# Delta-rule stage of a two-block kernel: convolution scratch, gate logarithm, Newton steps and low halves on other tiles and engines

## Chip, cores and metric

One core of a Trainium2 chip runs the whole program. The metric is the device time of one execution in microseconds (us). Three executions of the kernel before took 1437.9, 1439.62 and 1441.2 us; their median is 1439.62 us. Five engines work side by side, each through its own queue in order: TensorE (PE), VectorE (DVE), ScalarE (ACT), GpSimd (POOL) and SyncE (SP), which issues the loads of the weights.

## What is computed

Two blocks of a network over 256 tokens of width 1024, in float32. The first is a WKV mixer with a feed-forward part, the second a gated delta rule with a multiscale pool, followed by an expert layer (PEER). The change lies almost wholly in the delta rule of the second block:

```python
qkv = silu(causal_conv(qkv, conv_w))          # 4 taps, 3 x 512 channels
q, k = l2norm(q), l2norm(k)                   # 4 heads of 128
beta = sigmoid(b_gate)
g = -exp(a_log) * softplus(a_dec + dt_bias)   # the gate, 8 numbers a token row
# per chunk
g = cumsum(g); decay = exp(g_i - g_j)
t_mat = triangular_solve(I + strict(k_beta k^T * decay), I)
v_new = t_mat v_beta - (t_mat k_beta e^g) state
o = (q e^g) state + (q k^T * decay) v_new
state = state * e^{g_last} + k_decay^T v_new
# after it
o = rmsnorm(o) * silu(z);  x = x + [o, pool] @ w_out
```

## The kernel before

Activations lie with channels on the 128 partitions and the 256 tokens along the row. Every weight tile (128x1024) is multiplied in split precision: a rounded high half `whi` (line 210, ACT) and the rest as a low half `wlo` (line 223, DVE or POOL), so that a projection is 8 x 3 = 24 matmuls of 128x256 (lines 366 to 368). `Stream.split` makes both halves of the next weight tile; its argument says which engine makes the low half. Three buffers of each half exist, and two more after `widen` (line 238), which the feed-forward part calls (line 1194).

`delta` (from line 1230) is the stage of the change. Its work is two generators that `weave` (line 264) interleaves. `main` (line 1490) is the chain of the delta rule: `head` with the four convolutions of k and the gate (lines 1345 to 1357), the gate's running sum and decay (1495 to 1513), the norm of k (`rsqrt_steps`, line 400: a bit trick and three Newton steps), the matrix `N` (1529 to 1532), its inverse in 16-wide blocks (`inverse16`, from 589: 15 steps of a product, line 620, and a row sum, line 623), three levels of merging (1554 to 1610), then the two chunks (1611 to 1635). `filler` (line 1431) is everything that does not depend on the chain: 16 projections, four each for q, v, the pool `p` and the gate `z`, the convolutions that follow them (`conv_ops`, line 1278), the pool's windows (1406), and four steps of the output projection. `main` yields a number of microseconds from the list `YL`, and the filler is advanced by so much; a scheduler then sets each engine's order by priority and by its own estimate of times. So the order on an engine depends on these numbers, on which engine an operation is given to, and on which buffers must come free.

- `conv_ops` writes the scaled input to a tile `ct` (four buffers, line 1282) and the tanh to `th` (four buffers, line 1273). The four convolutions of k hold all four `ct` until their third tap; the first convolution of q takes the next.
- `gate_ops` (1299 to 1343) computes softplus through a series of log1p in `l8`, on 128x8 numbers, mostly on DVE.
- The last norm, of `o`, is `rsqrt_steps` again (line 1643), and the spreads of its result (line 1656) and the last four output steps wait for it.

`DSP`, `DSZ` and `GO` (lines 1384, 1385, 1450) name the engine of the low halves in the filler: before, POOL for all of them.

Of the kernel before, what the change touches and what calls it, by code (L numbers as in the profile page):

```python
# [9 lines left out]
F32 = mybir.dt.float32  # L10
# [5 lines left out]
AF = mybir.ActivationFunctionType  # L16
ALU = mybir.AluOpType
PSUM = bass.MemoryType.PSUM
P = 128
T = 256  # L20
# [142 lines left out]
NAR = 3  # L163
WX = 2
TY = [1.20, 8.92]
YL = [0.56, 0.64, 1.60, 3.20, 0.64, 0.72, 0.48, 0.80, 0.40, 1.92, 1.20, 0.16]
LEAD2 = 3000
LEAD3 = 3000
DSZ = 2
ORD = "qvpz"  # L170
FPRE = ["pb", "pa"]
DSP = 2
TOPK = 1.5
GSPLIT = 3
# [113 lines left out]
class Builder:  # L288
# [108 lines left out]
    def rsqrt(self, *a, **k):  # L397
        return drive(self.rsqrt_steps(*a, **k))

    def rsqrt_steps(self, src, n, mult, add=None, floor=None, out=None, pace=0.2):  # L400
        nc, sm = self.nc, self.s1
        V = nc.vector
        v, y, t = (sm.tile([P, 16], F32, name=k, tag=k)[:, 0:n] for k in ("rv", "ry", "rt"))
        y = y if out is None else out
        short = n <= 2 and floor is None
        k = 2.0 ** -28 if short else 1.0
        magic = 0x5EB759DF - 2 ** 31 if short else 0x5F3759DF
        parts = min(n, 2)
        w = n // parts
        cut = [tuple(ap[:, k * w:k * w + w] for ap in (src, v, y, t)) for k in range(parts)]  # L410
        cut = [(sp, vp if mult else sp, yp, tp) for sp, vp, yp, tp in cut]
        for sp, vp, yp, tp in cut if mult else []:
            if floor is not None:
                V.tensor_scalar(vp, sp, mult, floor, ALU.mult, ALU.max)
            else:
                V.tensor_scalar(vp, sp, mult * k, add * k, ALU.mult, ALU.add)
        yield pace
        for sp, vp, yp, tp in cut:
            V.tensor_single_scalar(yp.bitcast(I32), vp.bitcast(I32), 1, ALU.logical_shift_right)
        yield pace  # L420
        for sp, vp, yp, tp in cut:
            V.tensor_scalar(yp.bitcast(I32), yp.bitcast(I32), -1, magic, ALU.mult, ALU.add)
        if short:
            for c in (0.75, 0.1875, 3.0 / 1024):
                for sp, vp, yp, tp in cut:
                    V.scalar_tensor_tensor(tp, yp, vp, yp, ALU.mult, ALU.mult)
                for sp, vp, yp, tp in cut:
                    V.scalar_tensor_tensor(yp, tp, -c, yp, ALU.add, ALU.mult)
            return y
        for _ in range(3):  # L430
            yield pace
            for sp, vp, yp, tp in cut:
# [728 lines left out]
    def ffn(self, xs, pre, rs):  # L1161
        tc, nc, S = self.tc, self.nc, self.S
        V, A = nc.vector, nc.scalar
        with tc.tile_pool(name="ffn", bufs=1) as fp:
# [23 lines left out]
            for j in range(22):  # L1188
                fg = conv(j, nextp())
                if j == 6:  # L1190
                    self.delta_consts(fg[:, 0:1])
                fu = conv(22 + j, nextp())
                if j == 10:
                    S.widen(WX, self.nc.gpsimd)
                if j > 1:
                    acc = acc or [self.pa() for _ in range(4)]
                    self.out_step(acc, prev.pop(0), j == 2, False)
                    S.split()
                A.activation(fg, fg, AF.Gelu_apprx_tanh)
                V.tensor_tensor(fg, fg, fu, ALU.mult)  # L1200
                ah = fp.tile([P, T], F32R, name="ah", tag="ah", bufs=3)
                al = fp.tile([P, T], F32R, name="al", tag="al", bufs=3)
                self.split(ah, al, fg)
                prev.append((ah, al))
# [25 lines left out]
    def delta(self, xs, pre, rs):  # L1230
        tc, nc, i, S = self.tc, self.nc, self.i, self.S
        x = self.x
        V, A, G = nc.vector, nc.scalar, nc.gpsimd
        mm = nc.tensor.matmul
        b4 = lambda ps: ps.rearrange("p (c s) -> p c s", c=4)
        with tc.tile_pool(name="del", bufs=1) as dp:
            t4 = lambda n, dt=F32, tag=None: dp.tile([P, 4, T], dt, name=n, tag=tag or n)
            wpl, wbh, wbl, ab = self.wpl, self.wbh, self.wbl, self.ab
            ea = self.ea
            self.region.close()  # L1240
            for n in range(3):
                S.split((G, V, V)[n])
            k, q, v = t4("k"), t4("q"), t4("v")
            pp = t4("pp")
            z = t4("z")
            tri = self.con("tri")
            st = {}

# [17 lines left out]
                S.split(eng)  # L1266
                return ps

            def silu_ops(dst, src):
                d = {}  # L1270

                def tanh():
                    d["th"] = dp.tile([P, T], F32, name="th", tag="th", bufs=4)
                    A.activation(d["th"], src, AF.Tanh, scale=0.5)

                return tanh, lambda: V.scalar_tensor_tensor(dst, d["th"], 1.0, src, ALU.add, ALU.mult)

            def conv_ops(dst, ps, ch):
                d = {}

                def first():
                    d["t"] = dp.tile([P, T], F32, name="ct", tag="ct", bufs=4)
                    V.tensor_tensor(d["t"], ps, rs, ALU.mult)  # L1283
                    A.activation(dst, d["t"], AF.Copy, scale=self.par("conv2", 36 + ch))

                def tap(s):
                    V.scalar_tensor_tensor(dst[:, s:T], d["t"][:, 0:T - s], self.par("conv2", (3 - s) * 12 + ch),
                                           dst[:, s:T], ALU.mult, ALU.add)

                tanh, last = silu_ops(dst, dst)  # L1290
                return [first, lambda: tap(1), lambda: tap(2), lambda: (tap(3), tanh()), last]

            sp = dp.tile([P, 2, 8], F32, name="sp")
# [5 lines left out]
            def gate_ops():  # L1299
# [12 lines left out]
                                yr.unsqueeze(2).to_broadcast([P, 2, 8]), ALU.mult)  # L1312
                A.activation(beta, sp[:, :, 0:4], AF.Exp, scale=-1.0)
                yield
                V.tensor_tensor(z8, sp[:, :, 4:8], ab[:, 1:2, :].to_broadcast([P, 2, 4]), ALU.add)
                yield
                V.scalar_tensor_tensor(e8, z8, -1.0, z8, ALU.mult, ALU.min)
                A.activation(e8, e8, AF.Exp)
                yield
                V.tensor_scalar(beta, beta, 1.0, None, ALU.add)  # L1320
                V.tensor_scalar(z8, z8, 0.0, None, ALU.max)
                yield
                V.tensor_scalar(w8, e8, 2.0, None, ALU.add)
                V.reciprocal(beta, beta)
                yield
                V.reciprocal(w8, w8)
                V.tensor_scalar(bh, beta, 0.5, None, ALU.mult)
                yield
                V.tensor_tensor(e8, e8, w8, ALU.mult)
                yield  # L1330
                V.tensor_tensor(w8, e8, e8, ALU.mult)
                yield
                V.tensor_scalar(l8, w8, 1.0 / 15, None, ALU.mult)
                for n in (13, 11, 9, 7, 5, 3):
                    yield
                    V.scalar_tensor_tensor(l8, l8, 1.0 / n, w8, ALU.add, ALU.mult)
                yield
                V.scalar_tensor_tensor(l8, l8, 1.0, e8, ALU.add, ALU.mult)
                yield
                V.scalar_tensor_tensor(l8, l8, 2.0, z8, ALU.mult, ALU.add)  # L1340
                yield
                V.scalar_tensor_tensor(gt.rearrange("p (b h) -> p b h", b=2), l8, -1.0, ea.to_broadcast([P, 2, 4]),
                                       ALU.mult, ALU.mult)

            def head():
                V.tensor_scalar(dnh, self.par("dn"), 0.5, None, ALU.mult)
                go = gate_ops()
                next(go)
                kc = [conv_ops(k[:, h, :], ps, 4 + h) for h, ps in enumerate(pre)]
                for n in range(5):  # L1350
                    for ops in kc:
                        ops[n]()
                        if n:
                            next(go, None)
                        yield YL[0]
                for _ in go:
                    yield 0.2
# [113 lines left out]
            att = dp.tile([P, 8, P], F32, name="att", tag="Y2")  # L1471
            vb = dp.tile([P, 8, P], F32, name="vb")
            kd = dp.tile([P, 4, P], F32, name="kd")
            vn = dp.tile([P, 8, P], F32, name="vn")
            Sx = dp.tile([P, 4, P], F32, name="Sx")
            o = t4("o")
            oh, ol = t4("oh", F32R, "dec"), t4("ol", F32R, "N")

            G.memset(Y, 0.0)
# [10 lines left out]
            def main():  # L1490
# [23 lines left out]
                ss = self.pc()  # L1514
                l2sums(k, ss)
                yield YL[1]
                yield from self.rsqrt_steps(ss[:, 0:8], 8, 1.0, 4e-6, out=yk, pace=YL[11])
                V.tensor_tensor(byk, beta.rearrange("p b h -> p (b h)"), yk, ALU.mult)
                gk = [b4(self.pa()), b4(self.pa())]
                for tb in range(2):  # L1520
# [490 lines left out]
```

## Time and profile before

| | |
|---|---|
| runs of the kernel before | 1437.9, 1439.62, 1441.2 us |
| the profiled execution, its time | 1440.79 us |
| its span, first to last instruction | 1439.0 us |
| PE busy | 1356.5 us (94%) |
| DVE busy | 1022.3 us (71%) |
| ACT busy | 683.1 us (47%) |
| POOL busy | 322.6 us (22%) |
| delta stage, first gate product to the last sum into x | 433.5 to 588 us |

Busy time is the time in which an engine has an instruction in work; it counts an instruction that is held up as busy. The line PEclk of the page gives the TensorE clock that was granted, as a share of 2.4 GHz: 1.00 is 2.4 GHz and 0.50 is 1.2 GHz. In the timeline a row is a start, a length, an engine, a line of the code and what is written from what. Neighbouring rows of one engine overlap a little in the record, so what an instruction costs in a full queue is the distance from its start to the next start.

### The profile page before, as it was taken

What the parts mean: (1) busy time and instruction counts of PE and PEld (TensorE: products, weight loads), DVE (VectorE), ACT (ScalarE), POOL (GpSimd) and SP (SyncE); (2) the same over time, 40 slices, a digit from 0 to 9 for tenths busy, and PEclk for the clock granted to TensorE, in tenths of its full rate; (3) what the DMA queues carried; (4) which work ended last, traced back from release to release, by engine and by line L of the source; (5) the groups of instructions that cost most, each with busy time, mean ns of one, the idle gap of its engine ahead of it and who ended that gap; (6) DMA issues with size and microseconds to landing.
All of it is one profiled execution on the core that took longest, in us unless ns stands there. A gap on an engine that the chain in (4) does not pass through costs nothing.

```text
span 1439.0 us, 26837 instructions
## 1 busy us (share of the span) xinstructions
PE 1356.5 (94%) x10570; PEld 1264.0 (88%) x10570; DVE 1022.3 (71%) x2072; ACT 683.1 (47%) x1241; POOL 322.6 (22%) x232
## 2 busy tenths in 40 slices
PE   7989999999997887999979999999999999999998
PEld 6888989999987787999879999999998888888886
DVE  6865768888869876799992777777875555555554
ACT  3522455565554422465444554444444544554454
POOL 4511341210044632202341000000002222222221
PEclk9899999999999898999999999999999999999999
DMA  6231434665523211345435444444446655666653
GB/s 219 63 98 46 147 118 151 208 214 182 189 90 132 88 45 59 134 159 164 162 133 184 155 160 147 147 147 148 147 151 202 196 197 192 192 194 198 192 191 118
DMA packets 64318, 217.88 MB, mean 151 GB/s; under 512 B 10272, under 2 KB 11232, under 8 KB 64064
## 3 DMA queue, kind: packets, MB, share of 16 engines
q1 hardware_dynamic: 59376, 212.76, 44.9%
q0 software_dynamic: 976, 2.71, 0.7%
q8 instruction: 83, 1.36, 0.4%
q10 hardware_dynamic: 3840, 0.70, 0.4%
q14 instruction: 43, 0.35, 0.1%
HBM read 214.69 MB, written 1.44 MB: 150 GB/s over the span
## 4 chain that ended last, share of the span: by engine, by line
PE 69%; DVE 23%; issue 3%; ACT 2%; POOL 2%; DMA 1%; SPq 0%; ACTq 0%; DVEq 0%
PE pa L1919 24%; PE pb L366 10%; PE pb L368 9%; PE pb L367 9%; DVE wlo L223 5%; PE pa L367 2%; PE pa L366 2%; PE pa L368 2%; POOL wlo L223 1%; DVE x L1862 1%; DVE scr L1683 1%; DVE eg L1866 1%; PE pb L1873 1%; PE pa L1562 1%; DVE scr L1684 1%
## 5 line engine op out<-in xcount | busy, mean ns | idle before, releaser
L210 ACT ACTIVATE whi<-raw 128x1024 fp32r<-128x1024 f32 x396 | 418.2, 1058 | 555.6 <-PE pb L367 261.0
L223 DVE TENSOR_TENSOR wlo<-raw,whi 128x1024 fp32r<-128x1024 f32 x346 | 426.5, 1233 | 253.4 <-ACT whi L210 248.3
L366 PE MATMUL pb<-xnh,whi 128*128 128x256 f32 x1024 | 296.9, 290 | 13.8 <-DVE scr L1847 8.3
L368 PE MATMUL pb<-xnh,wlo 128*128 128x256 f32 x1024 | 290.7, 285 | 11.5 <-POOL wlo L223 6.8
L367 PE MATMUL pb<-xnl,whi 128*128 128x256 f32 x1024 | 290.1, 284 | 0.0
L1919 PE MATMUL pa<-whi,up 128*128 128x512 f32 x1024 | 274.5, 389 | 0.0
L1919 PEld LDWEIGHTS pa<-whi,up 128*128 128x128 f32 x1024 | 192.2, 188 | 39.8
L366 PEld LDWEIGHTS pb<-xnh,whi 128*128 128x128 f32 x1024 | 196.7, 192 | 18.2 <-PE pb L368 12.9
L368 PEld LDWEIGHTS pb<-xnh,wlo 128*128 128x128 f32 x1024 | 196.6, 192 | 13.2 <-POOL wlo L223 7.3
L223 POOL TENSOR_TENSOR wlo<-raw,whi 128x1024 fp32r<-128x1024 f32 x55 | 145.3, 2649 | 259.5 <-ACT whi L210 245.2
L367 PEld LDWEIGHTS pb<-xnl,whi 128*128 128x128 f32 x1024 | 196.9, 192 | 0.0
L366 PE MATMUL pb<-xh,whi 128*128 128x256 f32 x648 | 188.8, 291 | 4.3 <-DVE ct L1283 4.1
L368 PE MATMUL pb<-xh,wlo 128*128 128x256 f32 x648 | 185.6, 286 | 1.3 <-DVE wlo L223 1.3
L367 PE MATMUL pb<-xl,whi 128*128 128x256 f32 x648 | 186.0, 287 | 0.4
L1919 PE MATMUL pa<-wlo,up 128*128 128x512 f32 x512 | 158.2, 389 | 0.0
L494 POOL TENSOR_TENSOR up<-hb,up 128x256 fp32r<-128x256 f32 x32 | 45.9, 1435 | 409.3 <-ACT up L493 409.3
L366 PEld LDWEIGHTS pb<-xh,whi 128*128 128x128 f32 x648 | 125.2, 193 | 5.7 <-issue 4.3
L368 PEld LDWEIGHTS pb<-xh,wlo 128*128 128x128 f32 x648 | 124.8, 193 | 1.8 <-DVE wlo L223 1.5
L367 PEld LDWEIGHTS pb<-xl,whi 128*128 128x128 f32 x648 | 125.0, 193 | 1.4 <-DVE xl L560 1.0
L1919 PEld LDWEIGHTS pa<-wlo,up 128*128 128x128 f32 x512 | 96.1, 188 | 19.9
L494 POOL TENSOR_TENSOR up<-scr,up 128x256 fp32r<-128x256 f32 x32 | 47.1, 1472 | 127.0 <-ACT up L493 127.0
L367 PE MATMUL pa<-al,whi 128*128 128x256 f32 x176 | 49.0, 281 | 0.0
(529 smaller groups left out, 2267.0 us busy)
## 6 DMA issues: line engine op xcount, KB each, us to landing
raw<-down SPq DMA_DIRECT2D x128, 512.0 KB, 3.3
raw<-up SPq DMA_DIRECT2D x128, 512.0 KB, 4.3
raw<-w_in SPq DMA_DIRECT2D x46, 512.0 KB, 3.3
raw<-w_up SPq DMA_DIRECT2D x44, 512.0 KB, 3.6
raw<-w_down SPq DMA_DIRECT2D x22, 512.0 KB, 3.4
raw<-w_out SPq DMA_DIRECT2D x16, 512.0 KB, 3.3
raw<-w_query SPq DMA_DIRECT2D x16, 512.0 KB, 3.3
x<-xT SPq DMA_DIRECT2D x4, 256.0 KB, 5.3
```

What stands on the lines that cost most here:

```text
L210: nc.scalar.activation(hi, self.raw[self.nh], AF.Copy)
L223: e.tensor_tensor(lo[:, a:z], raw[:, a:z], hi[:, a:z], ALU.subtract)
L366: mm(ps, w[0], x[0], start=start, stop=False, **k)
L367: mm(ps, w[0], x[1], start=False, stop=False, **k)
L368: mm(ps, w[1], x[0], start=False, stop=stop, **k)
L494: (eng or self.nc.vector).tensor_tensor(lo, src, hi.bitcast(F32), ALU.subtract)
L1562: mm(out[:, h], lh[:, tb * 4 + h, :], self.halves(rh[:, tb * 4 + h, :], l, odd), start=True, stop=True)
L1683: V.max_index(idx[:, 0:8], vals[:, 0:8], src)
L1684: V.match_replace(t, vals[:, 0:8], src, NEG)
L1862: V.tensor_tensor(e1, iota, over(self.i1t), ALU.is_equal)
L1866: V.tensor_tensor(eg[m], eg[0], over(self.gp[m]), ALU.mult)
L1919: mm(acc[tb * 2 + hf], a[:, ts], b[:, hf * 512:hf * 512 + 512], start=False, stop=(e == 127 and lo == 1), skip_group_check=True)
```

## The change

- The four convolutions of k no longer use `ct` and `th`. Their scaled input lies in `vn` and their tanh in `o`, two tiles that the chain fills only much later.
- The gate's series becomes 22 POOL instructions on 128x8 numbers, with two reciprocals, one product and `bh` left on DVE and the cut at zero moved to ACT.
- The three Newton steps of the norm of k become 12 POOL instructions on 128x8 numbers (the argument `eng`); the norm of `o` stays as it was.
- All low halves of the filler are made by DVE (`DSZ`, `DSP`, `GO`), as is the first of three at the stage's start and the two of `widen` in the feed-forward part.
- `YL[0]`, the filler's share for each step of the k convolutions, goes from 0.56 to 0.2.

```diff
-YL = [0.56, 0.64, 1.60, 3.20, 0.64, 0.72, 0.48, 0.80, 0.40, 1.92, 1.20, 0.16]
+YL = [0.2, 0.64, 1.60, 3.20, 0.64, 0.72, 0.48, 0.80, 0.40, 1.92, 1.20, 0.16]
-DSZ = 2
+DSZ = 0
-DSP = 2
+DSP = 0
-GO = "GGGG"
+GO = "VVVV"
...
     def rsqrt_steps(self, src, n, mult, add=None, floor=None, out=None, pace=0.2, eng=None):
...
+        if eng:
+            v = v if mult else src
+            for _ in range(3):
+                yield pace
+                eng.tensor_tensor(t, v, y, ALU.mult)
+                eng.tensor_tensor(t, t, y, ALU.mult)
+                eng.tensor_scalar(t, t, -0.5, 1.5, ALU.mult, ALU.add)
+                eng.tensor_tensor(y, y, t, ALU.mult)
+            return y
...
-                    S.widen(WX, self.nc.gpsimd)
+                    S.widen(WX, V)
...
-                S.split((G, V, V)[n])
+                S.split(V)
...
+            o = t4("o")
+            vn = dp.tile([P, 8, P], F32, name="vn")
...
-                    d["t"] = dp.tile([P, T], F32, name="ct", tag="ct", bufs=4)
+                    d["t"] = dp.tile([P, T], F32, name="ct", tag="ct", bufs=4) if ct is None else ct
...
-                V.tensor_tensor(e8, e8, w8, ALU.mult)
-                yield
-                V.tensor_tensor(w8, e8, e8, ALU.mult)
-                yield
-                V.tensor_scalar(l8, w8, 1.0 / 15, None, ALU.mult)
-                for n in (13, 11, 9, 7, 5, 3):
-                    yield
-                    V.scalar_tensor_tensor(l8, l8, 1.0 / n, w8, ALU.add, ALU.mult)
...
+                G.tensor_tensor(e8, e8, w8, ALU.mult)
+                G.tensor_tensor(w8, e8, e8, ALU.mult)
+                G.tensor_scalar(l8, w8, 1.0 / 15, 1.0 / 13, ALU.mult, ALU.add)
+                yield
+                for n in (11, 9, 7, 5, 3, 1):
+                    G.tensor_tensor(l8, l8, w8, ALU.mult)
+                    G.tensor_scalar(l8, l8, 1.0 / n, None, ALU.add)
+                G.tensor_tensor(l8, l8, e8, ALU.mult)
...
+                vt = vn.rearrange("p (h a) t -> p h (a t)", h=4)
+                kc = [conv_ops(k[:, h, :], ps, 4 + h, vt[:, h, :], o[:, h, :]) for h, ps in enumerate(pre)]
...
-                yield from self.rsqrt_steps(ss[:, 0:8], 8, 1.0, 4e-6, out=yk, pace=YL[11])
+                yield from self.rsqrt_steps(ss[:, 0:8], 8, 1.0, 4e-6, out=yk, pace=YL[11], eng=G)
```

The order on POOL after the gate. `egb` and `N`, `dec` are the decay tiles, `pw` and `pp` the pool's windows, `rt`, `rv` and `yk` the norm of k. Before:

```order
L223 TENSOR_TENSOR wlo<-raw,whi 128x1024 x9
L1586 TENSOR_TENSOR egb<-egb,q 128x512
L1507 TENSOR_TENSOR N<-dec,con_del 128x512 x2
L1533 TENSOR_TENSOR dec<-dec,con_del 128x512
L223 TENSOR_TENSOR wlo<-raw,whi 128x1024
L1533 TENSOR_TENSOR dec<-dec,con_del 128x512
L1410 TENSOR_TENSOR pw<-pp 128x255
```

And now:

```order
L1590 TENSOR_TENSOR egb<-egb,q 128x512
L1416 TENSOR_TENSOR pw<-pp 128x255
L434 TENSOR_TENSOR rt<-rv,yk 128x8
L435 TENSOR_TENSOR rt<-rt,yk 128x8
L436 TENSOR_SCALAR rt<-rt 128x8
L437 TENSOR_TENSOR yk<-yk,rt 128x8
L434 TENSOR_TENSOR rt<-rv,yk 128x8
L435 TENSOR_TENSOR rt<-rt,yk 128x8
L1416 TENSOR_TENSOR pw<-pp 128x255
L436 TENSOR_SCALAR rt<-rt 128x8
L1416 TENSOR_TENSOR pw<-pw 128x254
L437 TENSOR_TENSOR yk<-yk,rt 128x8
```

The low halves are gone from this queue, and the Newton steps stand behind `egb`, which needs all of q, and between windows that each need a projection of the pool.

The order on DVE at the first steps of the inverse (`itmp` and `zd`; `dg` and a second buffer of it, shown with a number, are its input; `zt` and `z` belong to the gate z). Before, with the first z only eleven steps later, inside the inverse:

```order
L606 TENSOR_TENSOR dg<-dg,dg_5905 128x128
L1420 TENSOR_TENSOR pp<-pb,rbs 128x256
L620 TENSOR_TENSOR itmp<-zd,rep 128x4x2 x2
L623 TENSOR_REDUCE zd<-itmp 128x4 x2
...
L1401 TENSOR_TENSOR zt<-pb,rbs 128x256
L620 TENSOR_TENSOR itmp<-zd,rep 128x4x12 x2
```

And now:

```order
L615 TENSOR_TENSOR dg<-dg,dg_5775 128x128
L223 TENSOR_TENSOR wlo<-raw,whi 128x1024
L1287 SCALAR_TENSOR_TENSOR z<-th,zt 128x256
L1407 TENSOR_TENSOR zt<-pb,rbs 128x256
L223 TENSOR_TENSOR wlo<-raw,whi 128x1024
L1287 SCALAR_TENSOR_TENSOR z<-th,zt 128x256
L629 TENSOR_TENSOR itmp<-zd,rep 128x4x2 x2
L632 TENSOR_REDUCE zd<-itmp 128x4 x2
```

All 16 projections with their convolutions and 16 low halves now stand ahead of the inverse, and nothing stands between its 15 steps. On PE, likewise, the last z projection comes right ahead of the inverse's first matmuls, and no filler stands between those and the second chunk.

The order on DVE at the norm of `o` (`so` its sums, `yo` the result). Before:

```order
L1487 SCALAR_TENSOR_TENSOR so<-pc,qe 128x4
L419 TENSOR_SCALAR yo<-so 128x4
L422 TENSOR_SCALAR yo<-yo 128x4
L433 TENSOR_TENSOR rt<-so,yo 128x4
L436 SCALAR_TENSOR_TENSOR rt<-rt,yo 128x4
L439 SCALAR_TENSOR_TENSOR yo<-rt,yo 128x4
```

And now:

```order
L1491 SCALAR_TENSOR_TENSOR so<-pc,qe 128x4
L419 TENSOR_SCALAR yo<-so 128x4
L223 TENSOR_TENSOR wlo<-raw,whi 128x1024
L422 TENSOR_SCALAR yo<-yo 128x4
L442 TENSOR_TENSOR rt<-so,yo 128x4
L223 TENSOR_TENSOR wlo<-raw,whi 128x1024
L445 SCALAR_TENSOR_TENSOR rt<-rt,yo 128x4
L223 TENSOR_TENSOR wlo<-raw,whi 128x1024
L448 SCALAR_TENSOR_TENSOR yo<-rt,yo 128x4
```

Three low halves that POOL made beside these steps are now made by DVE between them.

## Rows read from the trace of the kernel before

**Rows 1.** Windows of the delta stage: length, busy per engine with counts, clock, DMA
```profile
core 0: us, PE busy (x) PEld busy (x) DVE busy (x) ACT busy (x) POOL busy (x), PEclk, DMA share, GB/s
433.50:485.70 52.20, 44.52 (x306) 43.74 (x307) 49.74 (x116) 25.29 (x57) 25.88 (x13) 0.84 0.33 112
...
516.50:557.40 40.90, 38.28 (x319) 37.80 (x318) 23.11 (x54) 7.25 (x13) 8.05 (x5) 0.96 0.11 39
557.40:588.00 30.60, 25.27 (x187) 24.12 (x187) 19.93 (x37) 10.11 (x16) 8.34 (x6) 0.89 0.28 98
```
**Rows 2.** Timeline of DVE and POOL where low halves meet convolutions and N
```profile
446.04 0.47 DVE L1287 SCALAR_TENSOR_TENSOR k<-ct,params,k 128x253 f32<-128x253 f32 x1
446.35 2.35 POOL L223 TENSOR_TENSOR wlo<-raw,whi 128x1024 fp32r<-128x1024 f32 x1 [3.11 <-ACT whi L210]
446.43 2.56 DVE L1287 SCALAR_TENSOR_TENSOR q<-ct,params,q 128x255 f32<-128x255 f32 x1
...
492.59 4.10 DVE L604 SCALAR_TENSOR_TENSOR dg<-N,con_del,dg 128x128 f32<-128x128 f32 x4
```
**Rows 3.** Groups of instructions on POOL and DVE, 425 to 590 us
```profile
L223 POOL TENSOR_TENSOR wlo<-raw,whi 128x1024 fp32r<-128x1024 f32 x21 | 50.3, 2406 | 59.5 <-ACT whi L210 55.8 <-PE pc L454 3.6
...
L1276 DVE SCALAR_TENSOR_TENSOR z<-th,zt 128x256 f32<-128x256 f32 x4 | 7.0, 1758 | 2.2 <-ACT th L1274 2.2
L223 DVE TENSOR_TENSOR wlo<-raw,whi 128x1024 fp32r<-128x1024 f32 x5 | 6.1, 1222 | 5.9 <-ACT whi L210 5.9
```
**Rows 4.** Waits of PE, 425 to 590 us: in total, times, longest
```profile
PE pb L446 <- DVE yo L439: 5.2, 1, 5.2
...
PE pb L366 <- DVE ct L1283: 4.1, 1, 4.1
```
**Rows 5.** Timeline of DVE in the inverse: first, stopped, a window's, last
```profile
500.18 0.57 DVE L620 TENSOR_TENSOR itmp<-zd,rep 128x8 f32<-128x8 f32 x2 [1.60 <-ACT rep L615]
...
507.60 2.10 DVE L620 TENSOR_TENSOR itmp<-zd,rep 128x52 f32<-128x52 f32 x1
...
510.74 0.41 DVE L1426 SCALAR_TENSOR_TENSOR pw<-pw,pp 128x256 f32<-128x256 f32 x1
...
512.71 0.34 DVE L623 TENSOR_REDUCE zd<-itmp 128x4 f32<-128x64 f32 x2
```
**Rows 6.** The merging chain: timeline of PE, and DVE at its end
```profile
464.93 3.76 PE L1500 MATMUL pa<-con_del,gt 128*128 128x128 f32 x16
...
518.18 2.00 PE L1562 MATMUL pa<-TT,N 128*128 128x64 f32 x16 [0.63 <-ACT TT L1552]
520.01 2.00 PE L1581 MATMUL pa<-q,k 128*128 128x128 f32 x16
...
557.42 0.69 DVE L1635 COPY o<-pa 128x512 f32<-128x512 f32 x1 [3.83 <-PE pa L1634]
```
**Rows 7.** Timeline at the norm of o, DVE and ACT
```profile
562.56 2.26 DVE L422 TENSOR_SCALAR yo<-yo 128x4 int32<-128x4 int32 x1
562.86 2.01 ACT L210 ACTIVATE whi<-raw 128x1024 fp32r<-128x1024 f32 x2 [0.55 <-PE pa L367]
...
570.63 0.16 DVE L439 SCALAR_TENSOR_TENSOR yo<-rt,yo 128x4 f32<-128x4 f32 x1
```
**Rows 8.** Windows around pauses of PE (columns as in Rows 1)
```profile
464.50:473.60 9.10, 9.10 (x43) 9.10 (x43) 7.26 (x17) 6.64 (x21) 3.46 (x2) 0.50 0.37 116
...
506.20:511.20 5.00, 0.00 (x1) 0.00 (x0) 5.00 (x17) 1.42 (x3) 3.01 (x3) 0.73 0.10 20
511.30:515.30 4.00, 4.00 (x17) 3.82 (x18) 3.96 (x15) 2.15 (x7) 2.44 (x3) 0.50 0.27 101
...
570.90:576.50 5.60, 5.51 (x23) 4.79 (x24) 2.84 (x8) 1.50 (x4) 0.00 (x0) 0.50 0.20 80
```
**Rows 9.** Groups of POOL by form, whole span: the smallest ones
```profile
L494 POOL TENSOR_TENSOR wbl<-wba,wbh 128x64 fp32r<-128x64 f32 x1 | 1.1, 1064 | 2.8 <-ACT wbh L493 2.8
...
L731 POOL MEMSET epos<- 128x16 f32 x1 | 0.1, 126 | 0.0
```

More of the change, by code (lines that the diff above doesn't have):

```diff
@@ L398, in rsqrt, with rsqrt_steps @@
         return drive(self.rsqrt_steps(*a, **k))
-    def rsqrt_steps(self, src, n, mult, add=None, floor=None, out=None, pace=0.2):
+    def rsqrt_steps(self, src, n, mult, add=None, floor=None, out=None, pace=0.2, eng=None):
         nc, sm = self.nc, self.s1
@@ L1267, in fproj, with silu_ops, conv_ops @@
                 return ps
-            def silu_ops(dst, src):
+            def silu_ops(dst, src, th=None):
                 d = {}
                 def tanh():
-                    d["th"] = dp.tile([P, T], F32, name="th", tag="th", bufs=4)
+                    d["th"] = dp.tile([P, T], F32, name="th", tag="th", bufs=4) if th is None else th
                     A.activation(d["th"], src, AF.Tanh, scale=0.5)
                 return tanh, lambda: V.scalar_tensor_tensor(dst, d["th"], 1.0, src, ALU.add, ALU.mult)
-            def conv_ops(dst, ps, ch):
+            def conv_ops(dst, ps, ch, ct=None, th=None):
                 d = {}
                 def first():
-                    d["t"] = dp.tile([P, T], F32, name="ct", tag="ct", bufs=4)
+                    d["t"] = dp.tile([P, T], F32, name="ct", tag="ct", bufs=4) if ct is None else ct
                     V.tensor_tensor(d["t"], ps, rs, ALU.mult)
@@ L1288, in tap @@
                                            dst[:, s:T], ALU.mult, ALU.add)
-                tanh, last = silu_ops(dst, dst)
+                tanh, last = silu_ops(dst, dst, th)
                 return [first, lambda: tap(1), lambda: tap(2), lambda: (tap(3), tanh()), last]
@@ L1314, in gate_ops @@
                 yield
-                V.tensor_tensor(z8, sp[:, :, 4:8], ab[:, 1:2, :].to_broadcast([P, 2, 4]), ALU.add)
-                yield
+                G.tensor_tensor(z8, sp[:, :, 4:8], ab[:, 1:2, :].to_broadcast([P, 2, 4]), ALU.add)
                 V.scalar_tensor_tensor(e8, z8, -1.0, z8, ALU.mult, ALU.min)
@@ L1319, in gate_ops @@
                 yield
-                V.tensor_scalar(beta, beta, 1.0, None, ALU.add)
-                V.tensor_scalar(z8, z8, 0.0, None, ALU.max)
-                yield
-                V.tensor_scalar(w8, e8, 2.0, None, ALU.add)
+                G.tensor_scalar(w8, e8, 2.0, None, ALU.add)
+                V.reciprocal(w8, w8)
+                G.tensor_scalar(beta, beta, 1.0, None, ALU.add)
                 V.reciprocal(beta, beta)
                 yield
-                V.reciprocal(w8, w8)
-                V.tensor_scalar(bh, beta, 0.5, None, ALU.mult)
-                yield
-                V.tensor_tensor(e8, e8, w8, ALU.mult)
-                yield
-                V.tensor_tensor(w8, e8, e8, ALU.mult)
-                yield
-                V.tensor_scalar(l8, w8, 1.0 / 15, None, ALU.mult)
-                for n in (13, 11, 9, 7, 5, 3):
-                    yield
-                    V.scalar_tensor_tensor(l8, l8, 1.0 / n, w8, ALU.add, ALU.mult)
[L1337 to L1343, printed above, removed]
+                G.tensor_tensor(e8, e8, w8, ALU.mult)
[6 more added lines that the diff above has]
+                G.tensor_tensor(l8, l8, e8, ALU.mult)
+                yield
+                A.activation(z8, z8, AF.Relu)
+                G.tensor_scalar(l8, l8, -2.0, None, ALU.mult)
+                G.tensor_tensor(l8, l8, z8, ALU.subtract)
+                G.tensor_tensor(gt.rearrange("p (b h) -> p b h", b=2), l8, ea.to_broadcast([P, 2, 4]), ALU.mult)
+                V.tensor_scalar(bh, beta, 0.5, None, ALU.mult)
             def head():
@@ L1348, in head @@
                 next(go)
-                kc = [conv_ops(k[:, h, :], ps, 4 + h) for h, ps in enumerate(pre)]
+                vt = vn.rearrange("p (h a) t -> p h (a t)", h=4)
+                kc = [conv_ops(k[:, h, :], ps, 4 + h, vt[:, h, :], o[:, h, :]) for h, ps in enumerate(pre)]
                 for n in range(5):
@@ L1473, in delta @@
             kd = dp.tile([P, 4, P], F32, name="kd")
-            vn = dp.tile([P, 8, P], F32, name="vn")
             Sx = dp.tile([P, 4, P], F32, name="Sx")
-            o = t4("o")
             oh, ol = t4("oh", F32R, "dec"), t4("ol", F32R, "N")
```

## The prediction

> **What bounds the kernel now.** I read the windows of the delta stage first, because all that the change touches there lies between 433.5 and 588 us. Ahead of the inverse the stage belongs to DVE: from 433.5 to 485.7 it is in work for 49.74 of 52.2 us, PE for 44.52 [rows 1]. From 516.5 to 557.4 PE is in work for 38.28 of 40.9 us [rows 1], but a part of that is filler that fills the waits of a chain.
>
> The timeline then says what DVE does with its time. A tap of a convolution takes 0.47 us; the next one, which begins just after POOL has begun a low half of 2.35 us, takes 2.56 [rows 2]. Nothing in a tap makes it five times as long: DVE stands until POOL is done. The reader is to see that a busy DVE here is partly a stopped DVE. The groups give the two prices of a low half: 21 on POOL at a mean of 2.4 us, five on DVE at 1.22 [rows 3]; in a full DVE queue the next start comes some 1.15 us after it, since records overlap.
>
> The waits show where PE pays: once 4.1 us for a `ct` and once 5.2 us for `yo` [rows 4].
>
> **The change, part by part.** The sum is made against the profiled execution's 1440.79 us.
>
> *Up to the inverse (433.5 to 500.2).* Twelve low halves of POOL go. Ten of them stop a DVE instruction with two inputs in SBUF, by about 2.1 us each; the tap at 446.43 is the pattern, and four `dg` rows that last 4.10 us at 492.59 are the last [rows 2]. That removes 21.5 us. DVE makes 16 low halves there instead, because all z projections are pulled ahead of the inverse: 16 x 1.15 = +18.4. The gate's and Newton's 34 small instructions leave DVE: 0.16 in the record like the one at 570.63 [rows 7], some 0.09 from start to start in a full queue: -3.1. The z products and two more windows of the pool come in ahead of the inverse, 11 at about 0.34: +3.7. The 34 small POOL instructions can now stop DVE in their turn, briefly; I put +2.5 for all. The sum is 0, with a range of -6 (POOL finds the gaps in which DVE reads PSUM, and DVE's own pauses shrink) to +6 (it doesn't, and PE's in-order pool products hold the projections behind them). So the k scratch and `YL[0]` are worth no term of their own: PE's wait of 4.1 us goes, but DVE sets the pace there, and late next is the running sum of the gate, which now stands after 3.6 q projections on PE.
>
> *The 15 steps of the inverse.* They run from 500.18 to 513.0, 12.9 us. One step lasts 2.10 us where its neighbours last 0.2, stopped by a low half [rows 5]; lesser stops of its neighbours add 1.5; six instructions of windows and z, of which the one at 510.74 is the last [rows 5], take 1.5. With these 4.9 us gone the steps need 8.0. Range -4 to -6.
>
> *Merging and chunks (516.5 to 557.4).* The four z products last 7.0 us in place of 4 x 0.42 [rows 3], so 5.3 us of stops leave, of which about 4 stand right ahead of sums that the merging waits for. Two z projections, 48 of the 319 matmuls in PE's 38.28 us [rows 1], or 5.7 us, leave the chain's gaps too; most of that filled waits, and I count 2.4. So -6.4. Against it stands the clock. PE will have nothing for some 8 us while the inverse runs. After the pause of 5.0 us at 506.2 the granted clock was 0.50 until PE had worked for 4.0 us, and after the one before 570.9 for 5.6 us [rows 8]; at this level 16 matmuls of 128x128 take 3.76 us and at the full one 2.00 [rows 6]. Before, a filler projection worked through the low stretch; now the chain does. Some 6 to 7 us of its matmuls at half rate cost +3.5 (bounds 0 and +8). Together -2.9.
>
> *The norm of o.* Three low halves on POOL stretch three DVE instructions to about 2.27 us each, the first at 562.56 [rows 7]; that is 6.2 us lost between `so` and the last Newton step at 570.63 [rows 7]. Now three low halves of 1.15 us stand there, 3.45 us, for -2.8. Their high halves are made at 562.86 to 564.9 [rows 7], so DVE hardly waits for them. PE's pause of 5.2 us [rows 4] becomes 2.4, and the clock, which was 0.50 for the 5.6 us after it [rows 8], may stay up. That would give back 2.8; I count half. Together -4.3 (-2.8 to -5.6).
>
> *At nothing:* the two low halves of `widen`, since they replace two that stop DVE by about as much (2.4 us if that cover fails); the cut at zero on ACT, which is in work for 7.25 to 25.29 us of these windows [rows 1].
>
> The sum is 0 - 4.9 - 2.9 - 4.3 = -12.1, so 1428.7 for such an execution. The median of the runs lies 1.2 below the profiled one, so I predict **1427.5 us**. With the parts' ranges not all at one end, this case alone spans 1419 to 1434.
>
> **Rivals.** *A: the clock stays low through the whole chain.* For it: from 464.5 to 473.6 the clock was 0.50 for all 9.1 us although PE was in work throughout [rows 8], on small float32 matmuls like the chain's. Against it: after 511.3 four us of dense matmuls were enough [rows 8], and by the order the merging begins with some 7 us of matmuls almost in a row. Its price: about 200 passes at 2.00/16 us or less [rows 6], 20 us on the path, doubled; less the 1.6 us that the chain lost before (a clock of 0.96 over 40.9 us [rows 1]), that is +18.4 in place of +3.5. The time is 1427.5 + 14.9 = 1442.
>
> *B: POOL's small instructions are late, and the kernel is slower.* The place is `gt`: PE takes it in order after 3.6 q projections, 86 matmuls of 0.119, about 443.7, and everything behind waits, all of v, p and z. The 19 POOL instructions from the reciprocals (about 2 us into the stage) to `gt` depend on each other, so they cost nothing only up to 0.42 us each; the 12 of Newton stand on the path to N. No row shows a POOL arithmetic instruction of 8 columns. From below, a memset of 16 columns takes 0.126 us; from above, a product of 64 columns took 1.064 [rows 9]. I take 0.3, nearer the memset by its size. At 1.064 the gate is 12 us late and Newton 9: 1427.5 + 21 = 1449. All gain is used up at 0.76 each, where 19 x 0.34 + 12 x 0.46 is 12.0. For it: DVE is never free there, and if POOL has to wait as DVE does in rows 2, a tap is added to each. Against it: a small instruction that waits only for the tap in work gets to 0.7 at most. On this the Trainium skill ("SBUF — State Buffer", "SBUF: two separate sides") has a rule that speaks against the change: the port pair that the two engines share is an exclusive lock, whoever starts first keeps it to its end, and the other fully blocks. By the rule a small POOL instruction that meets a DVE tap of 0.4 would cost 0.3 + 0.4 = 0.7, which makes the sum -12.1 + 10.1 = -2.0 and the time 1437.6. The trace shows DVE stopped by POOL, 2.56 us in place of 0.47; of POOL stopped by DVE no row here shows anything.
>
> *C: nothing moves much.* Low halves on DVE cost what the stops cost, the wait for `ct` only passes to the scratch of q and v, and the pool's windows, now between the Newton steps, hold the norm of k: the first part at +6, the clock at +8, so 1427.5 + 10.5 = 1438.
>
> **Chances.** Forecast 0.58, A 0.20 (1434 to 1446, since the clock may rise midway), B 0.15 (1436 to 1450), C 0.07 (1436 to 1441). About 0.2%, 2.9 us, is what a measurement of this kernel can tell from no change, so "the same" is 1436.7 to 1442.5. Faster: 0.57 of the forecast, 0.05 of A, 0.03 of B and C, 0.65. Same: 0.01 + 0.07 + 0.09 = 0.17. Slower: 0.08 + 0.10 = 0.18. The range that leaves out 2 in 10 takes in most of A and part of B: 1418 to 1445.
>
> **What would show it.** First part: the first inverse step at 494 to 506, and taps of 0.5 us instead of 2.5. Inverse: 15 steps in 8 us. Chain: the copy of `o` about 38 us after the merging's first matmul (516.5 to 557.42, 41, before), 50 and more under A, with the granted clock at 0.50 in it. Norm of `o`: about 5.3 us from L422 to the last step, not 8.1. B shows as PE waiting for `gt`, and as POOL rows starting more than 0.5 us apart in the gate. The forecast is wrong if the chain's clock doesn't rise or if a small POOL instruction costs over 0.7 us.

## The result and the profile after

| | before | changed |
|---|---|---|
| median, us | 1440.41 (4 runs) | 1423.71 (4 runs) |
| ratio to before | | 0.9874 [0.9833, 0.9915] |
| once more, beside B, J and K | 1440.78 (17 runs) | 1422.89 (4 runs), 0.9871 [0.985, 0.9892] |
| span of the profiled execution | 1439.0 | 1420.7 |

The kernel is 16.7 us faster, where 1427.5 (12.1 less) had been forecast. The windows of the delta stage show where; columns as in [rows 1]. The first two cover the time to the inverse, the third the inverse, the fourth merging and chunks, the fifth the norm of `o` and the output steps.

```profile
430.80:482.20 51.40, 48.06 (x389) 47.41 (x389) 47.92 (x103) 32.32 (x74) 27.71 (x48) 0.97 0.44 148
482.20:496.90 14.70, 12.82 (x106) 12.56 (x105) 13.81 (x34) 8.29 (x16) 4.16 (x6) 1.00 0.43 143
496.90:506.80 9.90, 1.14 (x12) 0.98 (x10) 9.69 (x65) 2.45 (x6) 1.99 (x2) 0.69 0.17 54
506.80:542.60 35.80, 34.44 (x267) 33.48 (x268) 15.23 (x46) 2.38 (x4) 0.00 (x0) 0.90 0.00 1
542.60:569.10 26.50, 23.96 (x182) 22.83 (x182) 16.27 (x39) 9.51 (x15) 0.82 (x2) 0.94 0.33 105
```

Ahead of the inverse PE is now in work for 60.9 of 66.1 us (before: 54.1 of 66.6 by the same view). In the inverse it has almost nothing, and in the chain no filler is left: 267 matmuls in place of 319 [rows 1].

DVE in the timeline: four taps in a row, then the inverse's first and last rows and its copy into `Z`.

```profile
436.55 1.66 DVE L1298 SCALAR_TENSOR_TENSOR k<-vn,params,k 128x254 f32<-128x254 f32 x4
...
496.94 0.25 DVE L629 TENSOR_TENSOR itmp<-zd,rep 128x8 f32<-128x8 f32 x2
...
504.30 0.34 DVE L632 TENSOR_REDUCE zd<-itmp 128x4 f32<-128x64 f32 x2
504.68 1.96 DVE L638 TENSOR_SCALAR Z<-zd,con_del 128x128 f32<-128x128 f32 x4
```

A tap takes 0.42 us from start to start, where the stopped ones took 2.56 [rows 2]. The 15 steps run from 496.94 to 504.64 without a stranger between them (12.9 us before [rows 5]).

PE at the head of the chain, and the copy of `o` on DVE at its end:

```profile
506.78 1.94 PE L1555 MATMUL pa<-con_base,Z 128*128 128x128 f32 x8 [8.76 <-DVE Z L638]
508.54 3.67 PE L1566 MATMUL pa<-TT,N 128*128 128x64 f32 x16
...
514.70 1.00 PE L1566 MATMUL pa<-Z,Y 128*128 128x64 f32 x8
...
542.62 0.69 DVE L1639 COPY o<-pa 128x512 f32<-128x512 f32 x1 [3.83 <-PE pa L1638]
```

After the pause of 8.76 us, 16 products take 3.67 us, 2.00 in [rows 6]: the lower clock level. From 514.7 on eight of them take 1.00. The waits of PE from 425 to 575 us, to set beside [rows 4]:

```profile
PE pa L1555 <- DVE Z L638: 8.8, 1, 8.8
PE pb L1460 <- POOL rt L435: 2.9, 1, 2.9
PE pb L455 <- DVE yo L448: 2.0, 1, 2.0
...
PE pa L1499 <- POOL gt L1347: 0.5, 1, 0.5
```

The wait for `ct` is gone and that for `yo` is 2.0 instead of 5.2. Next, POOL's small instructions in the gate; the one of 1.42 us lies beside a low half of DVE that starts at 439.63. Last, the other direction: a low half of DVE that starts beside a product of 128x512 on POOL.

```profile
433.50 0.20 POOL L1335 TENSOR_TENSOR e<-e,w 128x8 f32<-128x8 f32 x1 [0.32 <-DVE w L1331]
433.78 0.20 POOL L1336 TENSOR_TENSOR w<-e 128x8 f32<-128x8 f32 x1
...
439.50 1.42 POOL L1342 TENSOR_TENSOR l<-l,e 128x8 f32<-128x8 f32 x1
...
441.78 0.31 POOL L1347 TENSOR_TENSOR gt<-l,ea 128x8 f32<-128x8 f32 x1
```
```profile
452.00 1.36 POOL L1537 TENSOR_TENSOR dec<-dec,con_del 128x512 f32<-128x512 f32 x1
452.12 2.32 DVE L223 TENSOR_TENSOR wlo<-raw,whi 128x1024 fp32r<-128x1024 f32 x1
454.37 1.50 DVE L1298 SCALAR_TENSOR_TENSOR q<-ct,params,q 128x255 f32<-128x255 f32 x1
```

### The profile page after: what moved, and what is told of

It reads as the page before. It is cut to its first block, busy times and chain, and to the rows that moved or that the text cites. A ratio compares the mean times of both kernels' runs of the same rounds, so it can differ in the third digit from the quotient of the medians.

```text
span 1420.7 us, 26854 instructions
## 1 busy us (share of the span) xinstructions
PE 1347.7 (95%) x10570; PEld 1256.6 (88%) x10570; DVE 1002.0 (71%) x2060; ACT 683.5 (48%) x1242; POOL 284.3 (20%) x244
## 4 chain that ended last, share of the span: by engine, by line
PE 70%; DVE 21%; issue 3%; ACT 3%; POOL 3%; DMA 1%; SPq 0%; ACTq 0%; DVEq 0%; POOLq 0%
PE pa L1923 24%; PE pb L366 10%; PE pb L368 9%; PE pb L367 9%; DVE wlo L223 5%; PE pa L367 3%; PE pa L366 3%; PE pa L368 3%; PE pa L1566 1%; DVE x L1866 1%; DVE scr L1687 1%; DVE eg L1870 1%; PE pb L1877 1%; ACT whi L210 1%; POOL wlo L223 1%
## 5 line engine op out<-in xcount | busy, mean ns | idle before, releaser
L223 DVE TENSOR_TENSOR wlo<-raw,whi 128x1024 fp32r<-128x1024 f32 x368 | 457.5, 1244 | 252.7 <-ACT whi L210 251.0
L366 PEld LDWEIGHTS pb<-xnh,whi 128*128 128x128 f32 x1024 | 196.9, 192 | 18.2 <-PE pb L368 12.9
L223 POOL TENSOR_TENSOR wlo<-raw,whi 128x1024 fp32r<-128x1024 f32 x33 | 92.0, 2791 | 181.4 <-ACT whi L210 171.4
```

Of the source, the lines that this page charges most:

```text
L223: e.tensor_tensor(lo[:, a:z], raw[:, a:z], hi[:, a:z], ALU.subtract)
L366: mm(ps, w[0], x[0], start=start, stop=False, **k)
```

## The experiments

The start of the stage differs by up to 9 us (427.6 in I, 436.8 in F) between executions whose code ahead of it is the same, so the parts below are lengths, in us, of one profiled execution each, between the same landmarks. "To inverse": first gate product to the first inverse step. "Z": last step to the first matmul of merging. "Chain": from there to the copy of `o`. "Out": from there to the end of the last sum into `x`. The kernel before had a median of 1440.4 to 1440.8 us beside each group of runs.

| kernel | median (ratio to before, interval) | to inverse | 15 steps | Z | chain | out |
|---|---|---|---|---|---|---|
| before | 1440.4 | 66.7 | 12.9 | 3.5 | 40.9 | 30.4 |
| changed | 1423.7 (0.9874 [0.9833, 0.9915]) | 66.1 | 7.7 | 2.1 | 35.8 | 26.8 |
| A low halves alone | 1430.0 (0.9929 [0.9916, 0.9943]) | 70.4 | 11.7 | 2.4 | 36.1 | 26.9 |
| B the rest alone | 1440.3 (0.9999 [0.9988, 1.0011]) | 68.4 | 8.9 | 5.2 | 43.6 | 29.8 |
| C small ones on DVE | 1426.9 (0.9904 [0.9889, 0.992]) | 67.0 | 11.7 | 2.4 | 36.1 | 26.6 |
| D Newton on DVE | 1426.1 (0.9905 [0.9883, 0.9928]) | 68.1 | 7.7 | 2.1 | 36.0 | 26.5 |
| E no scratch | 1429.6 (0.9923 [0.9909, 0.9936]) | 66.8 | 11.8 | 2.1 | 36.8 | 27.6 |
| F no scratch, old `YL[0]` | 1434.2 (0.9963 [0.9937, 0.9989]) | 76.3 | 8.1 | 2.2 | 37.0 | 25.3 |
| G `GO` back | 1426.8 (0.9899 [0.9883, 0.9914]) | 66.1 | 7.7 | 2.1 | 36.7 | 29.4 |
| H `widen`, start back | 1426.9 (0.9914 [0.9886, 0.9942]) | 67.3 | 10.1 | 2.1 | 36.9 | 26.0 |
| I 50 matmuls added | 1419.5 (0.9862 [0.983, 0.9894]) | 66.0 | 7.7 | 2.1 | 36.6 | 26.3 |
| J 63 added | 1422.6 (0.9863 [0.9829, 0.9896]) | 66.1 | 7.7 | 2.1 | 32.2 | 26.7 |
| K 79 added | 1421.0 (0.9843 [0.9816, 0.9871]) | 66.0 | 7.7 | 2.1 | 32.2 | 25.3 |

The intervals of C, D, G and H overlap those of the changed kernel, so their costs of 2 to 3 us rest on the lengths more than on the medians. The profiled executions of F, I and J took 1438.3, 1428.2 and 1430.4 us, 4 to 9 us above their medians. In E to H the chain is 0.8 to 1.2 us longer because the granted clock stays at 0.50 for 9.3 to 9.7 us of it, 7.5 in the changed kernel; none of these edits aims at that.

**A, the low halves alone** (on the kernel before; B is the opposite, on the changed one).

```diff
-DSZ = 2
+DSZ = 0
-DSP = 2
+DSP = 0
-GO = "GGGG"
+GO = "VVVV"
-                    S.widen(WX, self.nc.gpsimd)
+                    S.widen(WX, V)
-                S.split((G, V, V)[n])
+                S.split(V)
```

> The kernel before with only the low halves moved to DVE (filler, first of three at the stage's start, widen); own scratch, gate, Newton and YL[0] stay as before. Theory (the low halves carry the gain, the small instructions and the scratch nothing): within 3 us of the changed kernel, 1424 to 1427, with taps of 0.5 us, 15 inverse steps in about 8 us and the steps of yo in 5.5 us. Rival (the scratch, which lets the q convolutions start, and the small instructions that leave DVE, carry at least a third): 1430 or more, with the first inverse step 4 us or more later than in the changed kernel.

1430.0: the rival. The chain and the last part are as short as in the changed kernel, but the time to the inverse is 3.7 us longer than before, although DVE is busy for no more of it (62.97 us against 62.58). A part of that buys something: PE makes 456 matmuls there, 381 before, some three projections more, which leave the inverse and the chain. And PE waits there, in its order:

```profile
PE pb L1454 <- DVE pw L1426: 8.0, 2, 4.6
...
PE pa L446 <- DVE byk L1518: 2.0, 1, 2.0
PE pb L366 <- DVE ct L1283: 1.3, 1, 1.3
```

**B, the rest alone.**

> The changed kernel with every low half back where it was before; scratch, gate and Newton on POOL and YL[0] as changed. From the runs so far scratch with YL[0] and the small instructions are worth some 8 us up to the merging, and the low halves the 2.6 us ahead of the stage, most of the chain's 5 and the norm's 3.5. Theory (the two groups add up): 1431 to 1434, the chain and the norm of o as long as before. Rival (both need a DVE that POOL doesn't stop, or POOL's queue with low halves makes gate and Newton late): 1437 or more, with POOL's gate instructions over 1 us apart and PE waiting for gt.

1440.3: nothing is gained, so the two groups don't add up. Against the changed kernel B loses 2.3 us up to the inverse, 4.2 in the inverse and right behind it, 7.8 in the chain and 2.9 after it. Some three projections are back in the chain (344 matmuls, 267 in the changed kernel), and the products of z are stopped there by low halves of POOL, as before the change:

```profile
526.76 2.38 POOL L223 TENSOR_TENSOR wlo<-raw,whi 128x1024 fp32r<-128x1024 f32 x1 [3.10 <-ACT whi L210]
527.02 2.39 DVE L1287 SCALAR_TENSOR_TENSOR z<-th,zt 128x256 f32<-128x256 f32 x1 [0.48 <-ACT th L1285]
```

POOL's small instructions stand in one queue with low halves that wait for their high half:

```profile
455.30 0.28 POOL L1341 TENSOR_SCALAR l<-l 128x8 f32<-128x8 f32 x1
458.52 2.51 POOL L223 TENSOR_TENSOR wlo<-raw,whi 128x1024 fp32r<-128x1024 f32 x1 [2.94 <-ACT whi L210]
...
468.37 0.20 POOL L1347 TENSOR_TENSOR gt<-l,ea 128x8 f32<-128x8 f32 x1
```

`gt` comes 37.2 us after the first gate product, 11.2 in the changed kernel. The longest wait of PE is now 9.0 us for `dg`, right ahead of the inverse; the wait for `gt` that the rival named is not there, since PE's order put `gt` late. That the late `gt` is what costs B is not shown: it comes 30.9 us after the first gate product before the change and 38.1 in C, which is 13 us faster than B.

**C and D, the small instructions.** D takes `eng=G` from the Newton call; C puts back the old `gate_ops` as well.

> The changed kernel with the gate logarithm and the Newton steps of k back on DVE; low halves, scratch and YL[0] as changed. Theory (34 small instructions are worth 3 us on DVE and cost as much by stops on POOL): within 3 us of the changed kernel, 1421 to 1427. Rival 1 (POOL's small instructions are late, since three of them took 1.0 to 1.4 us beside a low half of DVE, and PE waited 2.9 us and 0.5 us behind them): faster, 1418 to 1421, and PE's wait of 2.9 us at the pool product is gone. Rival 2 (freeing DVE was the gain): 1428 or more.

> The changed kernel with the 12 Newton instructions back on DVE and the gate on POOL as changed; all projections stand ahead of the inverse. Theory (Newton on POOL stood between the pool's windows for 8.1 us, and PE waited 2.9 us behind it and then worked 2.7 us at 0.50): 1 to 3 us faster than the changed kernel, 1421 to 1423, PE's waits at the pool products 2 us in all in place of 4.8. Rival (DVE is the bound there, and 18 instructions more cost it 2 us or more): 1425 to 1427.

C is 3.1 us slower, at the upper end of the theory, but not as the theory had it: in about the same time to the inverse it gets less done. The operations of two z projections, which the changed kernel has behind it by then, stand inside the steps (so too in A and E):

```profile
500.20 1.22 DVE L223 TENSOR_TENSOR wlo<-raw,whi 128x1024 fp32r<-128x1024 f32 x1
501.60 0.42 DVE L1287 SCALAR_TENSOR_TENSOR z<-th,zt 128x256 f32<-128x256 f32 x1
502.13 0.42 DVE L1413 TENSOR_TENSOR zt<-pb,rbs 128x256 f32<-128x256 f32 x1
503.00 1.23 DVE L223 TENSOR_TENSOR wlo<-raw,whi 128x1024 fp32r<-128x1024 f32 x1
```

D is 2.4 us slower at the median, 1.2 in the profiled execution, with 2.0 more ahead of the inverse: in favour of the rival, though the intervals overlap. The theory fell. The waits behind Newton that I wanted to be rid of came back as a wait of 3.7 us behind DVE's `rt`.

**E and F, the scratch.** E gives the k convolutions `ct` and `th` again, F also sets `YL[0]` to 0.56.

```diff
-kc = [conv_ops(k[:, h, :], ps, 4 + h, vt[:, h, :], o[:, h, :]) for h, ps in enumerate(pre)]
+kc = [conv_ops(k[:, h, :], ps, 4 + h  ) for h, ps in enumerate(pre)]
```

> The changed kernel without the own scratch of the k convolutions: they take ct and th again. Theory (no term of its own, DVE sets the pace there): within 3 us of the changed kernel, 1422 to 1427, though PE waits again some 4 us for a ct. Rival (that wait delays all projections, since PE takes them in order): 1428 or more, with the inverse 4 us later.

> The changed kernel without the scratch and with YL[0] back at 0.56: gate, Newton and low halves as changed. In the order of this kernel all z projections stand ahead of the inverse, as in the changed kernel, where without the scratch alone one of them fell into the inverse. Theory O (the 5.9 us lost without the scratch came with that order): within 2 us of the changed kernel, 1422 to 1426, the 15 steps in 7.7 us. Theory S (q's first convolution needs a ct that k holds, PE waits in order, and everything behind is late): 1427 to 1430, with PE's wait for ct back at 2 to 4 us and the inverse some 4 us later against the first gate product.

My theories fell in both. E costs 5.9 us with no wait for `ct` at all: 4.1 in the steps, the rest in the chain and behind it. F has its 15 steps nearly clean and costs more, 10.5. The timeline suggests why: the last product into `k` ends 37.9 us after the first gate product in F, 29.5 in A, 31.3 before, and 19.4 in the changed kernel. With shared `ct` either the convolutions of q crowd those of k (F, A, before) or, with a small `YL[0]`, k goes first (18.2) and q's work comes late (E: its first product at 26.8, 19.8 in the changed kernel). The scratch lets both go. This is read from the order of the rows; no run tests it alone.

**G, the norm of `o`.** Only `GO = "GGGG"`; nothing moves on PE, ACT and SP.

> The changed kernel with only the three low halves beside the norm of o back on POOL (GO); nothing else moves on PE, ACT or SP. Theory (a low half on POOL stops a DVE step of yo for its length): from so to the last step of yo 8.1 to 8.6 us in place of 5.5, PE's wait for yo 5 us in place of 2.0, the granted clock at 0.50 behind it for some 5 us in place of 3; time 3.5 us more, 1427. Rival (the steps overlap with POOL and the saving came from the chain ahead): within 1 us of the changed kernel.

```profile
547.81 2.26 DVE L422 TENSOR_SCALAR yo<-yo 128x4 int32<-128x4 int32 x1
550.11 2.27 DVE L442 TENSOR_TENSOR rt<-so,yo 128x4 f32<-128x4 f32 x1
552.41 2.26 DVE L445 SCALAR_TENSOR_TENSOR rt<-rt,yo 128x4 f32<-128x4 f32 x1
```
```profile
547.64 7.01 POOL L223 TENSOR_TENSOR wlo<-raw,whi 128x1024 fp32r<-128x1024 f32 x3 [41.93 <-ACT whi L210]
```

The cleanest run of the study: three low halves on POOL, one after the other, each hold one DVE step of 0.16 us for 2.26. From `so` to the last step 8.6 us, 5.5 in the changed kernel; the last part is 2.6 longer and the time 3.1; another 0.8 lies in the chain's clock.

**H, ahead of the stage.** `widen` and the first of three splits on POOL again.

> The changed kernel with the two low halves of widen and the first of three at the stage's start back on POOL. The prediction put them at nothing: within 1 us of the changed kernel. What the two traces showed (the first gate product 2.6 us earlier, of which some 0.7 lay ahead of the feed-forward part): 1 to 2.5 us slower, 1425 to 1426, with the step of rv stopped again by a low half of POOL.

3.2 us slower at the median. In the profiled execution the stage itself is 3.9 longer, since its order moved too (steps 10.1 us). Ahead of it, two lengths answer. From the first to the second block of residual sums (`nt`), which span the feed-forward part, it is 209.0 us, 209.4 before, 208.1 changed. From the step of `rv` to the gate product it is 7.03, 7.02 before, 6.04 changed. The step that low halves stop, in H and in the repeated changed kernel:

```profile
425.21 4.16 DVE L426 SCALAR_TENSOR_TENSOR rt<-ry,rv 128x1 f32<-128x1 f32 x2
```
```profile
426.13 1.95 DVE L426 SCALAR_TENSOR_TENSOR rt<-ry,rv 128x1 f32<-128x1 f32 x2
```

**I, J, K, the clock of the chain.** Matmuls on zeros, their result unused, in PE's pause; ten behind each third step, in J 13 more behind the last one, in K 16 more behind `so`.

```diff
+            if j in (1, 4, 7, 10, 13, 15):
+                w = self.s1.tile([P, 1], F16, name="warm", tag="warm", bufs=2)
+                A.activation(w, zd[:, n - 1, j:j + 1], AF.Copy, scale=0.0)
+                for _ in range(13 if j == 15 else 10):
+                    nc.tensor.matmul(ps[:, 0:T], w.to_broadcast([P, P]), w.to_broadcast([P, T]), start=True, stop=True)
```

> The changed kernel with 50 more matmuls of 128x256 on zeros, ten behind each third step of the inverse, in the pause of 8.8 us that PE has there; their result is not used. Theory (the chain's first 7.3 us run at 0.50 only because PE paused): the granted clock is 1.00 when the merging begins, its first sixteen 128x64 products take 2.00 us a group in place of 3.67, merging to the copy of o 32 to 33 us in place of 35.8, time 3 to 4 us less, 1420. Rival 1 (the added matmuls are too thin or too late and the clock stays at 0.50): 1424 to 1425. Rival 2 (ACT's small copies or the matmuls delay the inverse): 1425 or more.

> As the run with 50 added matmuls, with 13 more behind the last step of the inverse, so that PE pauses less than 1 us before the merging; in that run PE still paused 1.67 us and the granted clock was 0.50 from 503.4, right at the end of that pause, to about 513.3. Theory (a pause of 1.7 us right before the chain is what lowered it): 1.00 when the merging begins, from the first transpose of Z to the copy of o 32 to 33 us in place of 35.8, 3 to 4 us less than the changed kernel. Rival (the clock falls there whatever PE does before, since the added matmuls or the chain's own small ones don't hold it): 0.50 again for 7 us or more, no gain.

> As the run with 63 added matmuls, with 16 more behind so, in PE's wait of 2.0 us for yo. Theory: the granted clock stays at 1.00 where it was 0.50 for 3 us, another 1 to 1.5 us less, from the copy of o to the last sum into x 25 us in place of 26.5; 4 to 5 us less than the changed kernel in all, 1419. Rival (the added matmuls end after yo and delay its spreads): no gain at the norm, or a loss up to 1 us.

Windows of I at its last pause and behind it, then of K from the pause to the copy of `o`:

```profile
502.00:503.40 1.40, 0.00 (x0) 0.00 (x0) 1.30 (x4) 0.62 (x3) 1.16 (x2) 1.00 0.00 0
503.40:513.00 9.60, 9.55 (x45) 9.36 (x45) 2.53 (x9) 1.17 (x2) 0.00 (x0) 0.50 0.00 0
```
```profile
503.40:535.60 32.20, 30.79 (x267) 29.99 (x268) 15.43 (x46) 2.29 (x4) 0.00 (x0) 1.00 0.00 1
```

In I a pause of 1.67 us was left, and the chain behind it ran at 0.50 for 9.6 us and more: nothing gained there. J and K close it, the clock stays at 1.00, and the chain takes 32.2 us instead of 35.8. Not all of these 3.7 us is the clock: from the second product of `Z` and `Y` on (`pa<-Y,Z`, at 515.54 and 515.74), where the clock is 1.00 in both, J is still 0.7 shorter (changed kernel, then J; I and K have the 26.34 too, all others without filler in the chain 27.1 to 27.3).

```profile
515.54:542.62 27.08, 25.72 (x223) 24.98 (x223) 13.26 (x40) 1.21 (x2) 0.00 (x0) 1.00 0.00 1
515.74:542.08 26.34, 25.24 (x221) 24.64 (x221) 13.05 (x40) 1.22 (x2) 0.00 (x0) 1.00 0.01 1
```

So the low clock costs the changed kernel's chain 2.9 us, shown, and 3.7 at most. K also takes 1.5 us off the last part. Its stage is 5.4 us shorter than that of the changed kernel on the same chip, its median only 1.9 (1421.0 against 1422.9), and the intervals overlap: whether it beats the changed kernel is unclear. Behind the stage K loses 7.7 us again. Windows in the last stage, the repeated changed kernel and K:

```profile
1120.00:1360.00 240.00, 240.00 (x1060) 198.82 (x1059) 123.25 (x133) 120.23 (x176) 64.77 (x44) 1.00 0.58 194
```
```profile
1120.00:1360.00 240.00, 240.00 (x1030) 193.37 (x1029) 119.91 (x129) 116.92 (x172) 62.98 (x43) 1.00 0.57 189
```

PE is full in both at 1.00, yet K makes 1030 matmuls where the other makes 1060. All three profiled executions with added matmuls show it (344 or 345 in 80 us, 354 or 355 in all others); over the last stage that is some 8 us. It can't be an effect of the added matmuls having run, or not that alone: these executions differ from the others already ahead of the stage, in the opposite sense. The feed-forward part, measured as under H, takes them 204.8 to 206.0 us, the others with `widen` on DVE 207.5 to 208.2. Their times scatter widely (K: 1411.5 to 1423.0), so it may not be in every execution. I's lead in the table is not explained: in its profiled execution the chain did not get shorter, and no trace shows what its faster ones did. The cause is open.

## Why the prediction was right, and where it was not

The direction and the range held, the size roughly: 12.1 us forecast, 16.7 measured. By its own steps, in the profiled executions (18.3 less in span):

- **Up to the inverse, 0 forecast, -0.6 measured: right in part by luck.** The account of DVE held: it is busy for 61.7 us there, 62.6 before. The step that failed is "DVE sets the pace there", and with it "the k scratch and `YL[0]` are worth no term of their own". In A, DVE is busy for as long, yet the stretch is 3.7 us longer; by the waits, what ends last is a chain through k's convolutions, its norm and PE's fixed order, which is a reading and no test. Taking away the scratch costs 5.9 us (E), the small instructions 3.1 (C), each most of all as two z projections' work in the inverse.
- **The inverse, -4.9 forecast.** The steps gave 5.2. Missed was the copy into `Z` behind them, 1.3: 2.98 us on DVE before, 1.96 now, and PE was in filler until 516.5. All z work ahead of the inverse was read from the order rightly; that it hangs on three parts of the change at once was not.
- **Merging and chunks, -2.9 forecast, -5.1 measured.** The clock's share was +3.5 forecast and 2.9 to 3.7 by J. So the mis-sized term is the other one, -6.4: by the same subtraction it was -8.0 to -8.8. Up to 1.7 of that is a low stretch of the clock that the chain had before the change (0.50 from 546.1 to 549.5), which the prediction names under A and leaves out of this sum. Which of the other two pieces, the stops or the 48 filler matmuls, was larger than taken, no run separates. B shows that it comes with the low halves (chain 43.6 us).
- **The norm of `o`, -4.3 forecast, -3.6 measured.** The two terms, 2.8 and 1.4, add up to 4.2. The DVE part is right: 8.63 to 5.48 us, -3.2 (2.8 taken), and G shows it. The clock did not stay up: 0.51 from 555.6 to 558.7, in place of the 5.6 us of [rows 8].
- **"At nothing" was wrong for `widen` and the start: -2.6 ahead of the stage.** H shows 0.9 to 1.3 for `widen` and 1.0 for the start; the remaining 0.3 to 0.7 is scatter. For `widen`, "they replace two that stop DVE by about as much" failed by that length; what in the feed-forward part gives it was not followed up. The start had no term at all: there two low halves in a row on POOL held one step for 4.16 us, and a 1.95 with one 1.21 of DVE took their place.
- **Rival A fell.** 0.50 for the chain's first 7.5 us, then 1.00 to its end.
- **Rival B came at its low end.** A small POOL instruction takes 0.20 to 0.35 us and starts 0.28 to 0.43 after the one before; of the gate's 19, two were held for 1.02 and 1.42 by a low half of DVE. The gate took 8.6 us, 0.45 each against the 0.42 that were free, and PE waited 0.5 for `gt`. The rule of the Trainium skill ("SBUF — State Buffer", "SBUF: two separate sides") holds in both directions here: POOL waits for DVE (1.42 us in place of 0.28) and DVE for POOL (a low half of 2.32 in place of 1.22). But beside the taps of 0.42 the small instructions took 0.28 to 0.34 instead of 0.20, so in the gate the price of 0.7 that I derived from the rule did not come. The 12 of Newton did come near the rival: they took 8.1 us, 0.68 each, with four windows of the pool between them and two held for 1.2 by a low half of DVE, and PE waited 2.9 behind them. That is no loss against DVE, as D shows no gain without them. In B the gate was late, through the queue and not the lock: the low halves ahead of it.
- **Rival C fell**, "nothing moves much": 1438 against 1423.7. Its wait for `ct` did not pass on, and the pool's windows held the norm of k without making the stretch longer. B's 1440.3 is no case of it: the rival has the low halves on DVE, B has them on POOL.

## What to carry to other kernels

The parts of a change need not add up: the low halves alone gave 10.5 us, the rest alone nothing, both 17. Before an operation is given to another engine, read what stands ahead of it in that queue; where a long instruction waits there for a third engine, small dependent ones are late (the gate's 19 took 33.9 us in B, 8.6 in the changed kernel). A saving that empties an engine has a price where the emptied engine is next needed: the pause of 8.8 us that the clean inverse left PE was followed by 7.5 us at half clock, which cost the chain some 3 us.

## What the runs showed of the hardware that was not expected

- After a pause of 1.67 us ahead of the chain the granted clock was 0.50 (I); J and K, without that pause, kept 1.00. Before it PE had made 40 added matmuls in 4.70 us and, 0.44 later, ten in 1.29. The clock then stayed at 0.50 for 9.6 us and more of float32 products, 7.5 us in the changed kernel, though PE was in work nearly all of it.
- POOL and DVE hold each other in turns: a product of 128x8 on POOL lasts up to 1.42 us beside a low half of DVE, and one on DVE 2.26 in place of 0.16 beside a low half of POOL (G).
- A matmul of 128x512 in a full PE at a granted clock of 1.00 came every 0.226 us in most executions and every 0.233 in the three with added matmuls, 600 us after these. In the same three, a chain at 1.00 and the feed-forward part ahead of the added matmuls were shorter than elsewhere. Not explained.
